# Gate and up of two SwiGLUs with tokens stationary, and six of their 32 weight sections in seven half-size products instead of eight

## The chip, the cores and the metric

One core of a Trainium2 chip runs the whole block as one launch. The metric is the device time of that core in microseconds, as the median of the runs.

## The reference

The block takes 256 tokens of width 1,024 in float32 and returns the same shape. It has three sub-layers, each with a norm before it and a norm of its output, which is then added to x:

```python
x = x + 0.5 * rmsnorm(swiglu(rmsnorm(x, ffn1_pre_g), w_gate, w_up, w_down), ffn1_post_g)
h = rmsnorm(x, mix_pre_g)
z = h @ w_in                       # q, k, v, f | u, v_s | gates a, b
o_a = forgetting_attention(q, k, v, f, b_forget)
o_b = spatial_gating(gelu(u), gelu(v_s), ...)
x = x + rmsnorm((sigmoid(ga) * o_a + sigmoid(gb) * o_b) @ w_out, mix_post_g)
x = x + 0.5 * rmsnorm(swiglu(rmsnorm(x, ffn2_pre_g), ...), ffn2_post_g)
```

`swiglu(h, w_gate, w_up, w_down)` is `(silu(h @ w_gate) * (h @ w_up)) @ w_down` with 4,096 columns in gate and in up. These two, the first and the second SwiGLU, are what the change is about.

## The kernel before, in words

**Products.** Every large product is made of three float32r products. `split` (L77) makes the two parts of an operand: ScalarE casts it to `hi` (L78), VectorE subtracts that from the source and writes `lo` (L79). TensorE then adds hi·hi, hi·lo and lo·hi in one PSUM bank.

**Weights.** `load` (L90) brings 1 MiB, 128 partitions by 2,048 columns, into one of three buffers of the pool `raws`; SP's queue issues it. `piece` (L97) splits 1,024 of these columns into a pair of the pool `wts` (11 pairs), and `unit` (L106) is a load with its two pieces.

**Tokens.** The 256 tokens are two token tiles of 128. `xT` (L64) holds the normed x, turned and split: [partition, K tile of 8, token tile, hi | lo, 128]. `to_xT` (L154) fills half the columns of one token tile, with four transposes on TensorE and a split of their PSUM bank.

**SwiGLU** (`ffn`, L220). The 4,096 columns are 32 F tiles of 128. For each, `gate_up` (L232) holds the weights stationary (`wide`, L189): per K tile one product of 512 columns (both token tiles, hi and lo) and one of 256. Gate and up come out with F on the partitions, so `swiglu` (L212) needs no transpose: it adds the two halves (`wide_sum`), applies silu, multiplies and splits the result into `hT`, four F tiles in a buffer of the pool `big`. `down` (L265) is the product with the down weights, 6 products of 512 columns for an F tile and token tile, added up over all 32 F tiles in four PSUM banks `y`. It comes one F tile later in TensorE's queue; for the last ten F tiles (`DEFER`) token tile 1 waits until token tile 0 is done, so that tile 0's norm runs beside tile 1's products, and of these two (`KEEP`) come after tile 0 is turned into `xT`.

In the second SwiGLU the first four F tiles (`LEAD`) are done by token tile (`gate_up_of`, L240) with tokens stationary and turned by two transposes each. The transposes that put token tile 1 into `xT` stand after 72 of tile 0's 96 products of 256 columns.

**Mixer.** `proj` (L316) holds tokens stationary and moves 512 columns of weights. `section` (L327) does 1,024 columns for both token tiles at a time, `section_by_tile` (L341) first for one tile and then for the other. `section_by_tile` is used for v, gb and wo, next to the places where a token tile's norm is still under way.

**Norms.** `post_norm` (L179) and `pre_norm` (L167) follow each other for a token tile: ScalarE squares the halves of y (L139), VectorE multiplies y by the gain (`yg`, L182), GpSimd adds the two sums (L144) and takes the power -1/2 (L146) for `r`, VectorE updates x (L186); then squares of x, `r` again, and `hn` (L164), which is turned into `xT`.

**Order.** Each engine runs its queue in order. The program is written as one sequence, with `later(n, fn)` and `tick()` (L118, L121) putting a step off by n chunks of other work, and the framework sets each engine's queue from it.

Of the kernel before, what the change touches and what calls it, by code (L numbers as in the profile page):

```python
# [22 lines left out]
P = 128  # L23
# [6 lines left out]
H = 8  # L30
# [4 lines left out]
DEFER = 10          # last F tiles whose down product waits for token tile 1 until token tile 0 is done  # L35
KEEP = 2            # of these, the ones that come after token tile 0 is put into xT
LEAD = 4            # F tiles of the second SwiGLU that are done by token tile
WARM = 14           # idle products before the first data are there
FORGET, SCORES, TURN = 5, 3, 3  # chunks of other work before these steps (see later)
# [3 lines left out]
def block(ctx: ExitStack, tc: tile.TileContext, a: dict, out: bass.AP):  # L43
    nc = tc.nc
    const = ctx.enter_context(tc.tile_pool(name="const", bufs=1))
    raws = ctx.enter_context(tc.tile_pool(name="raws", bufs=3))
    wts = ctx.enter_context(tc.tile_pool(name="wts", bufs=11))
    gains = ctx.enter_context(tc.tile_pool(name="gains", bufs=2))
    mid = ctx.enter_context(tc.tile_pool(name="mid", bufs=12))
    big = ctx.enter_context(tc.tile_pool(name="big", bufs=3))  # L50
    small = ctx.enter_context(tc.tile_pool(name="small", bufs=4))
# [29 lines left out]
    def in_order(instructions):  # L81
        """Each engine takes its instructions of the list in the list's order."""
# [14 lines left out]
    def piece(raw, j, name, trace=None):  # L97
        r = raw[:, j * 1024:(j + 1) * 1024]
        hi = wts.tile([P, 1024], F32R, tag="hi", name=f"hi_{name}_{j}")
        lo = wts.tile([P, 1024], F32R, tag="lo", name=f"lo_{name}_{j}")  # L100
        done = split(hi, lo, r)
        if trace is not None:
            trace.extend(done)
        return hi, lo

    def unit(src, name):  # L106
        """1 MiB of weights, split into two pieces of 1024 columns."""
        raw = load(src, name)
        return [piece(raw, j, name) for j in range(2)]

    def view(piece, **kw):
        (k, n), = kw.items()
        return [w.rearrange("p (k n) -> p k n", k=n) for w in piece]

# [39 lines left out]
    def to_xT(t, c, src, name):  # L154
        """Half of the columns of a token tile into xT."""
# [33 lines left out]
    def wide(ps, lhs):  # L189
        """lhs(k): (hi, lo) [128, 128]."""  # L190
# [19 lines left out]
    marks = {}  # L210

    def swiglu(gate, up, hT, name):  # L212
        g = wide_sum(gate, f"g{name}")
        sg = mid_tile([P, NT, P], f"sg{name}")
# [472 lines left out]
```

## Time and profile before

| | |
|---|---|
| median of three runs | 766.69 us (766.54 to 766.77) |
| profiled execution, span | 766.7 us |
| TensorE busy | 755.1 us (98%), 3,974 products |
| VectorE busy | 486.4 us (63%) |
| ScalarE busy | 413.2 us (54%) |
| GpSimd busy | 17.4 us (2%) |
| read from HBM | 140.02 MB, 184 GB/s over the span |

The page gives no time of its own for the profiled execution beside its span, so the span is set against the runs. A product of TensorE is shown from its start to its modelled end, and neighbours overlap, so the length of one product is not the pace. The pace is read from the chain of waits in order of time, where a run of products stands with the time that the run took.

### The profile page before, as it was taken

To read this page: it belongs to the slowest core of one execution; us is meant where nothing else is said; L and a number is where in the kernel's file an instruction comes from. 1 tells how busy PE (TensorE), PEld (TensorE's weight loads), DVE (VectorE), ACT (ScalarE), POOL (GpSimd) and SP (SyncE) were. 2 spreads that over 40 slices of the span, in tenths; PEclk is the share of its full clock that TensorE was granted. 3 is DMA by queue.
4 is the path that set the end of the run, shared out by engine and by line. 5 is a ranking of instruction groups with operands and counts; after the bars stand their busy time and mean duration, and the time that the engine had idled before them with its cause. 6 is when DMAs were issued, how large, how long until landed. Compare 5 with 4: busy or idle time off the path is not lost.

```text
span 766.7 us, 10137 instructions
## 1 busy us (share of the span) xinstructions
PE 755.1 (98%) x3974; PEld 641.4 (84%) x3974; DVE 486.4 (63%) x731; ACT 413.2 (54%) x655; POOL 17.4 (2%) x32
## 2 busy tenths in 40 slices
PE   7999999999999999999999999999999999999996
PEld 4888888888888878888888888898888888888885
DVE  5885665666566586755486646875666566565652
ACT  4865555554545585754544434754555555554441
POOL 1000000000000020000010000200000000000000
PEclk8999999999999999999999999999999999999999
DMA  7885455555444366633346725555455545544401
GB/s 287 309 316 222 169 215 180 205 171 215 165 165 143 136 219 221 236 136 140 115 160 196 273 84 216 196 219 217 165 194 193 205 177 194 191 167 163 165 1 55
DMA packets 21983, 141.72 MB, mean 185 GB/s; under 512 B 3184, under 2 KB 3440, under 8 KB 5680
## 3 DMA queue, kind: packets, MB, share of 16 engines
q1 hardware_dynamic: 21936, 141.08, 51.0%
q8 instruction: 31, 0.51, 0.3%
q14 instruction: 16, 0.13, 0.1%
HBM read 140.02 MB, written 1.05 MB: 184 GB/s over the span
## 4 chain that ended last, share of the span: by engine, by line
PE 97%; DMA 1%; ACT 0%; DVE 0%; POOL 0%; issue 0%; SPq 0%; DVEq 0%; POOLq 0%; ACTq 0%
PE y L274 22%; PE g L194 15%; PE u L194 14%; PE u L195 8%; PE g L195 7%; PE qk L194 4%; PE gu L250 3%; PE v L321 3%; PE ga L321 3%; PE sv L321 3%; PE wo L321 3%; PE gb L321 3%; PE u L321 3%; PE qk L195 2%; DMA g_ffn_pre_g<-in_ffn_pre_g 1%; PE tp_f L158 1%
## 5 line engine op out<-in xcount | busy, mean ns | idle before, releaser
L79 DVE TENSOR_TENSOR lo_g<-raw_g,hi_g 128x1024 fp32r<-128x1024 f32 x128 | 155.9, 1224 | 88.0 <-ACT hi_g L78 87.8
L78 ACT CAST hi_g<-raw_g 128x1024 fp32r<-128x1024 f32 x128 | 133.3, 1049 | 73.8 <-PE y L274 60.0
L194 PE MATMUL u<-xT,hi_g 128*128 128x512 f32 x480 | 171.4, 394 | 0.0
L194 PE MATMUL g<-xT,hi_g 128*128 128x512 f32 x480 | 171.2, 395 | 0.0
L274 PE MATMUL y<-hi_d,hT 128*128 128x512 f32 x512 | 148.7, 392 | 0.0
L195 PE MATMUL u<-xT,lo_g 128*128 128x256 f32 x480 | 135.9, 283 | 0.0
L195 PE MATMUL g<-xT,lo_g 128*128 128x256 f32 x480 | 135.0, 281 | 0.0
L79 DVE TENSOR_TENSOR lo_d<-raw_d,hi_d 128x1024 fp32r<-128x1024 f32 x64 | 78.1, 1225 | 48.7 <-ACT hi_d L78 48.7
L274 PEld LDWEIGHTS y<-hi_d,hT 128*128 128x128 f32 x512 | 92.1, 188 | 19.1
L194 PEld LDWEIGHTS g<-xT,hi_g 128*128 128x128 f32 x480 | 90.5, 188 | 20.7 <-ACT hi_g L78 0.3
L194 PEld LDWEIGHTS u<-xT,hi_g 128*128 128x128 f32 x480 | 90.3, 188 | 20.6
L195 PEld LDWEIGHTS g<-xT,lo_g 128*128 128x128 f32 x480 | 90.4, 188 | 3.1 <-DVE lo_g L79 0.8
L195 PEld LDWEIGHTS u<-xT,lo_g 128*128 128x128 f32 x480 | 90.2, 188 | 0.1
L274 PE MATMUL y<-lo_d,hT 128*128 128x512 f32 x256 | 80.0, 391 | 0.0
L78 ACT CAST hi_d<-raw_d 128x1024 fp32r<-128x1024 f32 x64 | 66.7, 1049 | 16.8 <-PE u L194 9.7
L201 ACT ACTIVATE low_g<-g 128x256 f32<-128x256 f32 x60 | 23.0, 383 | 72.5 <-PE g L195 72.4
L274 PEld LDWEIGHTS y<-lo_d,hT 128*128 128x128 f32 x256 | 48.1, 188 | 10.6
L204 DVE TENSOR_TENSOR s_g<-g,low_g 128x256 f32<-128x256 f32 x60 | 25.4, 424 | 33.3 <-ACT low_g L201 33.3
L78 ACT CAST hT<-s_u 128x256 fp32r<-128x256 f32 x60 | 24.1, 402 | 30.9 <-DVE s_u L217 30.8
L215 ACT ACTIVATE sg<-s_g 128x256 f32<-128x256 f32 x60 | 25.0, 417 | 27.2 <-DVE s_g L204 27.2
L79 DVE TENSOR_TENSOR hT<-s_u,hT 128x256 fp32r<-128x256 f32 x60 | 25.2, 420 | 8.4 <-ACT hT L78 8.2
L217 DVE TENSOR_TENSOR s_u<-sg,s_u 128x256 f32<-128x256 f32 x60 | 25.5, 425 | 1.9
(324 smaller groups left out, 985.7 us busy)
## 6 DMA issues: line engine op xcount, KB each, us to landing
raw_g<-in_gu SPq DMA_DIRECT2D x63, 1024.0 KB, 4.8
raw_d<-in_dn SPq DMA_DIRECT2D x32, 1024.0 KB, 4.8
x<-in_x SPq DMA_DIRECT2D x2, 512.0 KB, 3.8
raw_g<-in_gu SPq DMA_DIRECT2D x2, 512.0 KB, 8.6
g_ffn_post_g<-in_ffn_post_g SPq DMA_DIRECT2D x2, 512.0 KB, 8.8
raw_v0a<-in_w_v SPq DMA_DIRECT2D x1, 1024.0 KB, 4.7
raw_v0b<-in_w_v SPq DMA_DIRECT2D x1, 1024.0 KB, 4.8
raw_v1a<-in_w_v SPq DMA_DIRECT2D x1, 1024.0 KB, 4.8
```

What stands on the lines that cost most here:

```text
L78: return [nc.scalar.copy(out=hi, in_=src), nc.vector.tensor_tensor(out=lo, in0=src, in1=hi.bitcast(F32), op=ALU.subtract)]
L79: nc.vector.tensor_tensor(out=lo, in0=src, in1=hi.bitcast(F32), op=ALU.subtract)]
L158: nc.tensor.transpose(out=ps[:, i * P:(i + 1) * P], in_=src[:, i * P:(i + 1) * P], identity=ident)
L194: nc.tensor.matmul(ps, lhsT=hi, rhs=xT[:, k], start=k == 0, stop=False, skip_group_check=True)
L195: nc.tensor.matmul(top, lhsT=lo, rhs=xT[:, k, :, 0, :], start=False, stop=k == KT - 1, skip_group_check=True)
L201: nc.scalar.activation(out=low, in_=pv[:, :, 1, :], func=AF.Copy, scale=scale)
L204: nc.vector.tensor_tensor(out=s, in0=pv[:, :, 0, :], in1=low, op=ALU.add)
L215: nc.scalar.activation(out=sg, in_=g, func=AF.Silu)
L217: nc.vector.tensor_tensor(out=u, in0=sg, in1=u, op=ALU.mult)
L250: nc.tensor.matmul(ps[:, i * 256:(i + 1) * 256], lhsT=xT[:, k, t, xs, :], rhs=w, start=k == 0 and q == 0, stop=k == KT - 1 and q == 2, ski ...
L274: nc.tensor.matmul(ys[t][c], lhsT=hT[:, t, xs, :], rhs=w[:, c * 512:(c + 1) * 512], start=f == 0 and q == 0, stop=f == NF - 1 and q == 2)
L321: nc.tensor.matmul(ps, lhsT=xT[:, k, t, xs, :], rhs=w, start=k == 0 and q == 0, stop=k == KT - 1 and q == 2)
```

## The change

**Weights.** Gate and up come as blocks of 1,024 columns, four blocks (`NB`) of each, cut like the mixer's sections into quarters of 512 columns by half of K: `src[c, kh]`, 1 MiB each. `quarter` loads one and splits it in one step of 2,048 columns (`parts_of`), where `piece` took 1,024. The pool `raws` has five buffers in place of three, `wts` four pairs of 2,048 columns in place of 11 of 1,024.

**Products.** All of gate and up now hold tokens stationary, 512 columns to a product. For each block, gate is done first and then up. Gate of block 0 is done by token tile; the other sections are `section` or, for up of blocks 1 to 3 of both SwiGLUs (`FAST1`, `FAST2`), `fast`. `fast` takes the section as a 2 by 2 product: token tiles by column halves, with K in two halves. Where `section` makes eight products of one token tile, one quarter and half of K (12 matmuls each), `fast` makes seven, out of sums of quarters (`add`, in place in the raw buffers) and sums of parts of xT (`sums`, once for each SwiGLU), and puts the four results together with `mixed`. Both kinds of sums are on VectorE. The parts of xT's sums are split like any operand.

**Transposes.** h is now [tokens, columns]. For each block, token tile and column half, `turn` transposes it in four steps on TensorE and splits the result into `hT`.

**Order.** The down products of block b - 1 are spread over the steps of block b. The transposes of token tile 1 into `xT` in the second SwiGLU (`before`) come after two steps of block 0's gate, that is 24 products. In the first SwiGLU the last eight F tiles less two (`HOLD`) are done for tile 0 first and then for tile 1. At the start all four parts of xT are made before the first gate section, and its first quarter is split in two halves.

```diff
-    raws = ctx.enter_context(tc.tile_pool(name="raws", bufs=3))
-    wts = ctx.enter_context(tc.tile_pool(name="wts", bufs=11))
+    raws = ctx.enter_context(tc.tile_pool(name="raws", bufs=5))
+    wts = ctx.enter_context(tc.tile_pool(name="wts", bufs=4))
...
+    def sums(name):
+        kept = big.tile([P, NT, 2, 512], F32, tag="b", name=f"kept_{name}")
+        for t in range(NT):
+            for c in range(2):
+                hi, lo = [xT[:, c * 4:c * 4 + 4, t, i, :].bitcast(F32) for i in range(2)]
+                nc.vector.tensor_tensor(out=kept[:, t, c].rearrange("p (k c) -> p k c", c=P), in0=hi, in1=lo, op=ALU.add)
...
+    def fast(src, name, parts, done):
...
+        b11 = get(0, 0)
+        a = bank(f"{name}A")
+        product(a, lhs_x(0, 0), b11, "p1", True)
+        p1 = mid_tile([P, 512], f"{name}p1")
+        nc.scalar.copy(out=p1, in_=a)
+        yield
+        b12 = get(1, 0)
+        add(b11, b11, b12)
+        c = bank(f"{name}C")
+        product(c, lhs_s(0), b11, "p5", True)
+        yield
+        b22 = get(1, 1)
+        add(b11, b11, b22)
+        b = bank(f"{name}B")
+        product(b, lhs_s(1), b11, "p6", True)
+        u2 = mixed("u2", b, p1, ALU.add)
+        w = mixed("w", c, u2, ALU.subtract)
+        yield
+        add(b12, b12, b22)
+        b21 = get(0, 1)
+        product(a, lhs_x(1, 0), b21, "p2", False)
+        done(0, 0, a)
+        yield
+        d = bank(f"{name}D")
+        product(d, lhs_s(2), b12, "p7", True)
+        done(1, 1, mixed("y11", w, d, ALU.subtract))
+        yield
+        product(c, lhs_s(3), b22, "p3", False)
+        done(0, 1, mixed("y01", c, u2, ALU.subtract))
+        yield
+        add(b11, b11, b21)
+        product(d, lhs_x(1, 1), b11, "p4", False)
+        done(1, 0, mixed("y10", d, u2, ALU.add))
+        yield
...
+            for gen, _ in steps:
+                for _ in gen:
+                    at += 1
+                    if b == 0 and at == 2 and before:
+                        before()
+                    if b == 0 and at == 9 and quick:
+                        parts.append(sums(f"f{n}"))
+                    tick()
+                    while had > 0 and gone < had * at // total:
+                        f = side.pop(0)
+                        down(f, 0)
+                        down(f, 1)
+                        gone += 1
...
-    ffn(2, LEAD, done2, lambda t: turn[t]())
+    ffn(2, FAST2, done2, before=lambda: turn[1]())
```

The next three pieces are of the engines' queues, each row an instruction with its line, what it writes and reads, and the shape.

VectorE's queue in the middle of the first SwiGLU, before: F tiles 18 and 19, with gate and up weights `g1_22`, `g1_23` and down weights `d1_20` split beside them.

```order
L204 TENSOR_TENSOR s_g1_18_1535<-g1_18_1499,low_g1_18_1533 128x256
L79 TENSOR_TENSOR lo_d1_20_0_1767<-raw_d1_20_1764,hi_d1_20_0_1766 128x1024
L79 TENSOR_TENSOR lo_d1_20_1_1771<-raw_d1_20_1764,hi_d1_20_1_1770 128x1024
L204 TENSOR_TENSOR s_u1_18_1541<-u1_18_1500,low_u1_18_1539 128x256
L217 TENSOR_TENSOR s_u1_18_1541<-sg1_18_1537,s_u1_18_1541 128x256
L79 TENSOR_TENSOR lo_g1_22_0_1789<-raw_g1_22_1786,hi_g1_22_0_1788 128x1024
L79 TENSOR_TENSOR hT1_16_1384<-s_u1_18_1541,hT1_16_1384 128x2x128
L204 TENSOR_TENSOR s_g1_19_1604<-g1_19_1568,low_g1_19_1602 128x256
L79 TENSOR_TENSOR lo_g1_22_1_1793<-raw_g1_22_1786,hi_g1_22_1_1792 128x1024
L79 TENSOR_TENSOR lo_g1_23_0_1858<-raw_g1_23_1855,hi_g1_23_0_1857 128x1024
L204 TENSOR_TENSOR s_u1_19_1610<-u1_19_1569,low_u1_19_1608 128x256
L217 TENSOR_TENSOR s_u1_19_1610<-sg1_19_1606,s_u1_19_1610 128x256
```

The change puts in that engine's queue the beginning of up of block 2 (`lo_u1_2p1` to `u1_2w`):

```order
L84 TENSOR_TENSOR lo_u1_2p1_1106<-raw_u1_200_1102,hi_u1_2p1_1105 128x2048
L289 TENSOR_TENSOR raw_u1_200_1102<-raw_u1_200_1102,raw_u1_210_1123 128x2048
L289 TENSOR_TENSOR raw_u1_210_1123<-raw_u1_210_1123,raw_u1_211_1161 128x2048
L84 TENSOR_TENSOR lo_u1_2p5_1128<-raw_u1_200_1102,hi_u1_2p5_1127 128x2048
L289 TENSOR_TENSOR raw_u1_200_1102<-raw_u1_200_1102,raw_u1_211_1161 128x2048
L84 TENSOR_TENSOR lo_d1_12_1146<-raw_d1_12_1143,hi_d1_12_1145 128x2048
L84 TENSOR_TENSOR lo_u1_2p6_1166<-raw_u1_200_1102,hi_u1_2p6_1165 128x2048
L289 TENSOR_TENSOR raw_u1_200_1102<-raw_u1_200_1102,raw_u1_201_1186 128x2048
L84 TENSOR_TENSOR lo_u1_2p2_1189<-raw_u1_201_1186,hi_u1_2p2_1188 128x2048
L84 TENSOR_TENSOR lo_u1_2p7_1219<-raw_u1_210_1123,hi_u1_2p7_1218 128x2048
L293 TENSOR_TENSOR u1_2u2_1181<-u1_2B_1164,u1_2p1_1121 128x512
L293 TENSOR_TENSOR u1_2w_1183<-u1_2C_1126,u1_2u2_1181 128x512
```

Where subtractions of 1,024 columns stood between short steps of 256, there are now passes over 2,048 columns, seven subtractions and four sums to a section (the first four and three of them here), and the first two combinations `u2` and `w` stand behind five subtractions of the section and one of down weights.

VectorE's queue before, from the last subtractions of `g2_3` to token tile 1's `hn_f21` at the entry into the second SwiGLU (`xT` rows are tile 0's):

```order
L79 TENSOR_TENSOR lo_g2_3_0_4504<-raw_g2_3_4501,hi_g2_3_0_4503 128x1024
L79 TENSOR_TENSOR xT_82<-tp_f200_4365,xT_82 128x4x128
L79 TENSOR_TENSOR xT_82<-tp_f201_4372,xT_82 128x4x128
L79 TENSOR_TENSOR lo_g2_3_1_4508<-raw_g2_3_4501,hi_g2_3_1_4507 128x1024
L79 TENSOR_TENSOR lo_g2_4_0_4700<-raw_g2_4_4697,hi_g2_4_0_4699 128x1024
L182 SCALAR_TENSOR_TENSOR yg_pm11_4398<-wo11_4352,g_mix_post_g_4193 128x512
L186 SCALAR_TENSOR_TENSOR x_79<-yg_pm10_4396,r_pm1_4400,x_79 128x512
L186 SCALAR_TENSOR_TENSOR x_79<-yg_pm11_4398,r_pm1_4400,x_79 128x512
L79 TENSOR_TENSOR lo_g2_4_1_4704<-raw_g2_4_4697,hi_g2_4_1_4703 128x1024
L164 SCALAR_TENSOR_TENSOR hn_f210_4413<-x_79,r_f21_4410,g_ffn2_pre_g_4195 128x512
L164 SCALAR_TENSOR_TENSOR hn_f211_4415<-x_79,r_f21_4410,g_ffn2_pre_g_4195 128x512
```

And with the change, the same place:

```order
L184 SCALAR_TENSOR_TENSOR yg_pm10_3610<-wo10_3541,g_mix_post_g_3423 128x512
L84 TENSOR_TENSOR lo_g2_001_3642<-raw_g2_001_3639,hi_g2_001_3641 128x2048
L84 TENSOR_TENSOR xT_88<-tp_f200_3579,xT_88 128x4x128
L84 TENSOR_TENSOR xT_88<-tp_f201_3586,xT_88 128x4x128
L84 TENSOR_TENSOR lo_g2_010_3689<-raw_g2_010_3686,hi_g2_010_3688 128x2048
L184 SCALAR_TENSOR_TENSOR yg_pm11_3612<-wo11_3566,g_mix_post_g_3423 128x512
L188 SCALAR_TENSOR_TENSOR x_85<-yg_pm10_3610,r_pm1_3614,x_85 128x512
L188 SCALAR_TENSOR_TENSOR x_85<-yg_pm11_3612,r_pm1_3614,x_85 128x512
L84 TENSOR_TENSOR lo_g2_011_3695<-raw_g2_011_3692,hi_g2_011_3694 128x2048
L166 SCALAR_TENSOR_TENSOR hn_f210_3627<-x_85,r_f21_3624,g_ffn2_pre_g_3425 128x512
L166 SCALAR_TENSOR_TENSOR hn_f211_3629<-x_85,r_f21_3624,g_ffn2_pre_g_3425 128x512
```

A subtraction stands ahead of `yg_pm11` and another between the new x and `hn_f210` in both; with the change they are of 2,048 columns.

TensorE's queue before, around token tile 1's transposes `tp_f210` and `tp_f211` there:

```order
L250 MATMUL gu2_2_0_4511<-lo_g2_2_1_4498,xT_82 128x256
L250 MATMUL gu2_2_0_4511<-hi_g2_2_1_4497,xT_82 128x256
L158 MATMUL tp_f210_4536<-ident_83,hn_f210_4413 128x128 x4
L158 MATMUL tp_f211_4543<-ident_83,hn_f211_4415 128x128 x4
L250 MATMUL gu2_2_0_4511<-hi_g2_3_0_4503,xT_82 128x256
L250 MATMUL gu2_2_0_4511<-lo_g2_3_0_4504,xT_82 128x256
```

And with the change:

```order
L217 MATMUL g2_000_3645<-lo_g2_001_3642,xT_88 128x512
L217 MATMUL g2_000_3645<-hi_g2_001_3641,xT_88 128x512
L160 MATMUL tp_f210_3672<-ident_89,hn_f210_3627 128x128 x4
L160 MATMUL tp_f211_3679<-ident_89,hn_f211_3629 128x128 x4
L217 MATMUL g2_001_3698<-hi_g2_010_3688,xT_88 128x512
L217 MATMUL g2_001_3698<-lo_g2_010_3689,xT_88 128x512
```

The transposes keep their place behind token tile 0's products, but stand behind 24 of 512 columns in place of 72 of 256.

## Rows read from the trace of the kernel before

**Rows 1.** The page: busy time of each engine, and the chain by engine.
```profile
PE 755.1 (98%) x3974; PEld 641.4 (84%) x3974; DVE 486.4 (63%) x731; ACT 413.2 (54%) x655; POOL 17.4 (2%) x32
...
PE 97%; DMA 1%; ACT 0%; DVE 0%; POOL 0%; issue 0%; SPq 0%; DVEq 0%; POOLq 0%; ACTq 0%
```
**Rows 2.** Busy time by stretch: us, each engine (instructions), granted clock, DMA share, GB/s.
```profile
0.00:14.00 14.00, 9.35 (x31) 5.43 (x32) 6.31 (x14) 5.21 (x9) 1.92 (x8) 0.83 0.86 303
14.00:27.00 13.00, 12.96 (x67) 10.77 (x67) 10.44 (x14) 10.29 (x16) 0.00 (x0) 0.92 0.82 313
27.00:755.00 728.00, 727.27 (x3855) 620.98 (x3854) 466.86 (x701) 396.37 (x628) 14.62 (x22) 1.00 0.51 183
```
**Rows 3.** The chain in order of time: start us, us, engine, what, line, count.
```profile
26.50 2.75 PE y L274 x12
...
201.92 2.75 PE y L274 x12
...
271.50 0.24 ACT junk_p L139
...
443.84 16.73 PE gb L321 x72
...
487.40 0.87 PE tp_f L158 x8
...
491.06 8.65 PE gu L250 x72
...
500.59 2.85 PE gu L250 x24
...
503.66 5.70 PE gu L250 x48
```
**Rows 4.** Timeline, 10 to 15 us: start, us, engine, line, operation [idle before, releaser].
```profile
10.13 3.65 PE L158 MATMUL tp_f<-ident,hn_f 128*128 128x128 f32 x16 [3.44 <-DVE hn_f L164]
...
11.87 0.69 DVE L79 TENSOR_TENSOR xT<-tp_f,xT 128x512 fp32r<-128x512 f32 x1 [1.10 <-ACT xT L78]
...
13.69 0.79 PE L194 MATMUL g<-xT,hi_g 128*128 128x512 f32 x1
```
**Rows 5.** Groups by line and shape: busy us, mean ns of one, idle before.
```profile
L79 DVE TENSOR_TENSOR lo_g<-raw_g,hi_g 128x1024 fp32r<-128x1024 f32 x128 | 155.9, 1224 | 88.0 <-ACT hi_g L78 87.8
L78 ACT CAST hi_g<-raw_g 128x1024 fp32r<-128x1024 f32 x128 | 133.3, 1049 | 73.8 <-PE y L274 60.0 <-PE u L194 10.7 <-DMA raw_g<-in_gu 1.8
...
L79 DVE TENSOR_TENSOR xT<-tp_f,xT 128x512 fp32r<-128x512 f32 x8 | 5.2, 686 | 1.7 <-ACT xT L78 1.7
...
L78 ACT CAST xT<-tp_f 128x512 fp32r<-128x512 f32 x8 | 4.4, 590 | 7.7 <-PE tp_f L158 7.7
```
**Rows 6.** Timeline, GpSimd's step L144 and the VectorE subtractions beside it.
```profile
277.58 1.22 DVE L79 TENSOR_TENSOR lo_v1a<-raw_v1a,hi_v1a 128x1024 fp32r<-128x1024 f32 x1
277.79 1.19 POOL L144 TENSOR_SCALAR r_mx<-ms_mx 128x1 f32<-128x1 f32 x1 [3.84 <-ACT junk_mx L139]
...
289.53 0.30 POOL L144 TENSOR_SCALAR r_mx<-ms_mx 128x1 f32<-128x1 f32 x1 [2.46 <-ACT junk_mx L139]
...
490.93 2.35 DVE L79 TENSOR_TENSOR lo_g<-raw_g,hi_g 128x1024 fp32r<-128x1024 f32 x2
...
492.22 1.23 POOL L144 TENSOR_SCALAR r_pm<-ms_pm 128x1 f32<-128x1 f32 x1 [6.73 <-ACT junk_pm L139]
```
**Rows 7.** Timeline, VectorE and TensorE at the two entries.
```profile
279.65 1.42 DVE L164 SCALAR_TENSOR_TENSOR hn_mx<-x,r_mx,g_mix_pre_g 128x512 f32<-128x512 f32 x2 [0.84 <-POOL r_mx L146]
280.55 1.29 PE L158 MATMUL tp_mx<-ident,hn_mx 128*128 128x128 f32 x8 [0.70 <-DVE hn_mx L164]
...
485.53 1.42 DVE L164 SCALAR_TENSOR_TENSOR hn_f<-x,r_f,g_ffn_pre_g 128x512 f32<-128x512 f32 x2 [0.86 <-POOL r_f L146]
...
493.20 0.68 DVE L182 SCALAR_TENSOR_TENSOR yg_pm<-wo,g_mix_post_g 128x512 f32<-128x512 f32 x1
...
497.53 1.41 DVE L164 SCALAR_TENSOR_TENSOR hn_f<-x,r_f,g_ffn_pre_g 128x512 f32<-128x512 f32 x2 [0.85 <-POOL r_f L146]
```

More of the change, by code (lines that the diff above doesn't have):

```diff
@@ L95, in load, with parts_of, quarter @@
         return raw
[L97 to L103, printed above, removed]
-        return hi, lo
[L106 to L113, printed above, removed]
+    def parts_of(raw, name, parts=1, trace=None):
+        hi = wts.tile([P, 2048], F32R, tag="hi", name=f"hi_{name}")
+        lo = wts.tile([P, 2048], F32R, tag="lo", name=f"lo_{name}")
+        for c in range(0, 2048, 2048 // parts):
+            cs = slice(c, c + 2048 // parts)
+            done = split(hi[:, cs], lo[:, cs], raw[:, cs])
+            if trace is not None:
+                trace.append(done)
+        return hi, lo
+    def quarter(src, name):
+        return parts_of(load(src, name), name)
     pending = []
@@ new lines, in section_by_tile @@
+    def section_by_tile(src, name, done, first=None):
+        ws = {}
+        for t in range(NT):
+            for c in range(2):
+                for kh in range(2):
+                    if (c, kh) not in ws:
+                        ws[c, kh] = first if first and (c, kh) == (0, 0) else quarter(src[c, kh], f"{name}{c}{kh}")
+                ps = bank(f"{name}{t}{c}")
+                for kh in range(2):
+                    proj(ps, t, ws[c, kh], kh, 0, 1)
+                    if kh == 1:
+                        done(t, c, ps)
+                    yield
@@ L265, in down, with ffn @@
+    marks = {}
+    def ffn(n, quick, done, before=None, after=None, first=None):
+        gs, us, dn = a[f"g{n}"], a[f"u{n}"], a[f"dn{n}"]
+        hTs, ys, downs, sgs = {}, {}, {}, {}
         def down(f, t, cs=(0, 1)):
             if f not in downs:
-                downs[f], downs[f + 1] = unit(dn[f // 2], f"d{n}_{f}")
+                w = quarter(dn[f // 2], f"d{n}_{f}")
+                for i in range(2):
+                    downs[f + i] = [v[:, i * 1024:(i + 1) * 1024] for v in w]
             if t not in ys:
@@ L288, in ffn @@
-        late = []
-        nxt = 0
-        for f in range(lead, NF):
-            gate_up(f, first if (n, f) == (1, 0) else unit(gu[f], f"g{n}_{f}"))
-            if f == lead and lead:
-                turns[-1]()
-            while nxt < f:
-                down(nxt, 0)
-                if nxt < NF - DEFER:
-                    down(nxt, 1)
-                else:
-                    late.append(nxt)
-                nxt += 1
-        late.append(NF - 1)
-        down(late[0], 1)
-        down(late[1], 1)
@@ L305, in ffn @@
+        for f in side[:HOLD]:
+            down(f, 0)
+            down(f, 1)
+            tick()
+        late = side[HOLD:]
+        for f in late:
+            down(f, 0)
         done(0, ys[0])
-        for e in late[2:-KEEP]:
-            down(e, 1)
-        if n == 1:
-            turned(0)
+        for f in late[:-KEEP]:
+            down(f, 1)
+        if after:
+            after()
         for c in range(2):
-            for e in late[-KEEP:]:
-                down(e, 1, (c,))
+            for f in late[-KEEP:]:
+                down(f, 1, (c,))
@@ L476, in mixer, with columns @@
         kept = forget()
-        section_by_tile(a["w_v"], "v", v_done)
+        run(section_by_tile(a["w_v"], "v", v_done))
+        parts = sums("mx") if FASTM else None
+        def columns(src, name, done):
+            run(fast(src, name, parts, done) if name in FASTM else section(src, name, done))
         oA = attention(v, *kept)
-        ws = raws.tile([P, H, P], F32, tag="raw", name="ws")
+        ws = aux.tile([P, H, P], F32, tag="aux", name="ws")
         nc.vector.memset(ws[64:128, :, 0:64], 0.0)
@@ L526, in u_done @@
             later(2 + t, mix)
[L528 removed]
+        columns(a["w_u"], "u", u_done)
         def ga_done(t, c, ps):
@@ L577, in block @@
     nc.sync.dma_start(out=ident, in_=a["ident"])
-    trace, rs, first = [], [], []
+    trace, rs = [], []
     for t in range(NT):
```

235 lines of the change are left out of this document (119 added, 116 removed).

## The prediction

> **What bounds the kernel now.** First the page's busy shares and its chain of waits [rows 1]: TensorE is busy for 755.1 of 766.7 us and the chain lies on it for 97%, while VectorE is busy for 63% and ScalarE for 54%. Then the table by stretch [rows 2]: from 27 to 755 us TensorE is idle for 0.73 us in all, and its granted clock is 1.00, that is 2.4 GHz; in 0 to 14 and 14 to 27 it is lower. So a change counts by what it does to TensorE's queue, plus every wait that it opens there. Third, the chain in order of time [rows 3] gives the pace. From the y group of 12 at 26.50 to the one at 201.92 are 21 F tiles, 8.35 us each, 2.75 of which is the down product: gate and up of one F tile take 5.60 us. With tokens stationary, 72 products take 16.73 us, 232.4 ns each. The four F tiles done by token tile take 8.65 + 2.85 + 5.70 and once more 5.70, 22.9 us. Eight transposes take 0.87 us, 109 ns each.
>
> **TensorE, the matrix products.** Removed: 60 x 5.60 + 22.9 = 358.9 us. Added: ten sections of 96 products and six of 84, 1,464 products with tokens stationary, at 232.4 ns: 340.2 us. Sum: **-18.7**. The half-size products alone are six times 12 products, 16.7 us of it; the change of form is worth 2.0. Down products and the mixer's matrix products are the same in number.
>
> **TensorE, transposes.** h now comes out as [tokens, columns] and must be turned: 128 transposes in place of 8, so 120 x 109 ns = **+13.0**. They stand in TensorE's queue, which is full, so nothing hides them. Running sum: -5.7.
>
> **Start of the first SwiGLU.** Before, the first product starts at 13.69 [rows 4] and two F tiles are done at 26.50: 11.2 us of work, so the loss is 1.6 and the effective start 15.3. Now the first gate section runs token tile 0 over all four weight quarters, 12 products (2.8 us) each, and each quarter needs a 2,048-column split. VectorE's subtraction took 1.22 us for 1,024 columns and 0.69 for 512 [rows 5], 1.05 ns a column: 2.30 for 2,048. ScalarE's cast, 1.05 and 0.59: 1.95. On VectorE from 11.87 [rows 4], with the halves of the first quarter ready at about 14.1 and 16.0: two xT halves (17.2), one `kept` sum (17.9), a quarter (20.2), two sums (21.6), a quarter (23.9), a sum (24.6), the last quarter (26.9). After that 55 products are left, 12.8 us: the 96 products end at 39.7, less 22.3 of work is an effective start of 17.4, **+2.1**. Bounds: 0 if the sums yield, +4 if a load also comes late.
>
> **The two entries.** Here a token tile's norm stands between TensorE's last product and its next transposes, and VectorE's queue has a weight subtraction between x and hn in both kernels, twice as long now. It matters twice, because GpSimd's step waits too [rows 6]: r at L144 took 0.30 us alone, but 1.19 and 1.23 when a subtraction ran, ending 0.18 and 0.17 after that subtraction's own end (278.80 and 493.28).
> I take the hold to last to the subtraction's end, since both of these did; if it stayed at the 0.9 us that they cost, the entries below would be some 2 us cheaper in all.
> The Trainium skill (SBUF — State Buffer, section "Who interferes with whom") says that a VectorE instruction with two SBUF inputs and a GpSimd instruction that reads SBUF exclude each other for the whole instruction. The two rows agree with it; no run here shows a 2,048-column hold yet.
>
> Into the mixer: before, y's tile 0 ends at 271.50, hn starts at 279.65 and the transposes at 280.55 [rows 3, 7], with 36 y products (8.2 us) as cover and 0.70 us idle. Now the cast between the two squares is 0.9 longer, the subtraction then runs to about 280.2, r follows it, the transposes start near 281.8: **+1.3**.
>
> Into the second SwiGLU, tile 0: before, hn starts at 485.53 [rows 7] and the transposes are due at 487.40, so 1 us is to spare. Now the subtraction ends near 486.6, r at 487.4, hn at 488.15 and its second half at 488.85: +1.15.
> Tile 1: before, `wo` ends at 491.06, hn starts 6.5 us later, and 72 products of 8.65 us cover it [rows 3, 7]. Now `before()` is called after two steps, 24 products or 5.6 us. VectorE comes late to `yg_pm11` (it has hn, two quarters and two xT halves first, to 495.3, where before it was there at 493.20 [rows 7]); r is held until then, x is done at 497.4, the next subtraction at 499.65, r at 500.4, hn at 501.2. `wo` ends at 492.2 with the wait of tile 0, the 24 products at 497.8: idle 3.65. Together **+4.8**. Bounds: 2 (hold as in the rows, cast not in the way) to 7 (a 2.30 subtraction more).
>
> **The six seven-product sections.** VectorE has 11 passes over 2,048 columns (seven subtractions, four sums), 25.3 us, 13 passes over 512 columns (combinations, gate times up, hT) at 0.69, 9.0, and two down quarters, 4.6: 38.9 us. TensorE has 84 + 48 products and three groups of transposes there, 32.0. VectorE alone would be 6.9 us short in each. But it works ahead: by the order it runs five of the passes after the gate's last quarter and before the first weights that must wait for a buffer of this section, 11.5 us, and with four weight buffers and all four raw quarters loaded it can. So 27.4 remain against 32.0. The thin places are the transposes in and after the section, which wait for a combination that stands behind a subtraction: my walk leaves them 0.1 to 0.3 us. I take 0.4 a section, **+2.4**; the bounds are 0 and 6.9 a section, and the value lies near the low end because the cover is counted in the order.
>
> **Nothing:** ScalarE (seven casts of 1.95 and a copy in 32 us), the loads (same bytes; rows of the page show no product waiting for one after the start), the tail (same last products, same norm), and five buffers of raw weights for three. If VectorE is late, the first of these to bind is a load, since a raw quarter is freed by its last subtraction.
>
> **Sum:** -5.7 + 2.1 + 1.3 + 4.8 + 2.4 = +4.9. The profiled execution's span is 766.7, the runs' median 766.69, so the two need no correction: **771.6 us**, slower by 0.6%. About 0.2%, 1.5 us, is what a measurement of this kernel can tell from no change.
>
> **Rivals.**
> *Faster: the entries and sections wait for nothing more.* If the subtractions that stand before hn are done while VectorE would wait anyway, the terms 1.3, 4.8 and 2.4 go: 763.1. For it: ScalarE and VectorE have 46 and 37% idle, and the runs of before show no TensorE wait at the second entry. Against: the order puts the subtraction before hn. It decides where TensorE's idle time at the second entry is under 1 us.
> *VectorE is the bound in the seven-product sections.* If the lead is lost (a weight buffer or a raw quarter comes free late), up to 6.9 a section; with half of it, 6 x 3.5 = 21 more: 790. For it: 38.9 against 32.0. Against: the five passes ahead.
> *TensorE's clock falls in the new waits.* Rows: the clock is 0.83 in 0 to 14, where TensorE waits 3.44 us before its first transposes [rows 2, 4], 0.92 in 14 to 27 and then 1.00, also through the 0.70 us wait. At 0.92 over 13 us a wait costs 1.0 more; at the start and the second entry that is 2: 773.6, more if sections wait as well.
> The Trainium skill (TensorE: Matmul & The Clock Gate, section "HAM oscillation — how this bites in real kernels") states that idle gaps of TensorE bring its clock down and that each then starts cold; of the waits here, the trace shows it for the 3.44 us only, and for 0.70 us not.
> That the change doesn't do what it says is excluded: the order counts 504 products on the seven-product line.
>
> **How the numbers follow.** Forecast 0.56, of which the low ends (entries 3 to 4, sections 0 to 1, start 1: 765 to 767) leave 0.14 within 0.2%; faster rival 0.24; VectorE rival 0.13; clock 0.07. Faster 0.24, same 0.14, slower 0.62. The forecast's own range is 765 to 778; taking in most of the faster rival, down to a start that loses nothing more against 1 us left at the entries (762), and a small part of the VectorE rival (half a section in all, +3 on 778) gives 762 to 781.
>
> **What would show it.** Right: about 340 us of gate and up products at 232 ns, 128 transposes at 109 ns, TensorE idle some 3 to 4 us around the second entry with r at L146 as releaser one step back, and a few tenths per section before L371. Wrong: idle time of TensorE above 2 us in each seven-product section, waiting for VectorE's lo (the second rival); no idle at the entries (the first); a granted clock below 1.00 in the middle of the kernel (the third); or a pace of the 512-column products other than 232 ns, each nanosecond of which is 1.5 us.

## The result and the profile after

| | before | after |
|---|---|---|
| median | 766.73 us (766.54 to 766.98, 4 runs) | 771.93 us (769.38 to 773.91, 4 runs) |
| ratio | | 1.0061, 95% interval 1.0036 to 1.0085 |
| profiled execution | span 766.7 us | span 767.6 us, its time 769.38 us |

The change makes the kernel slower by 0.6%. The profiled execution is the fastest of the four. A run's time lies some 1.8 us above its span (769.38 and 767.6 here, 767.0 and 765.2 in a run of before beside the experiments), so the profiled execution of before, span 766.7, took about 768.5 us, 1.8 above the median of its runs. Two differences are therefore to be explained: 0.9 us between the two traces, and the rest between the trace of after and the median of its runs.

First the page of after, the busy time of each engine, against [rows 1]:

```profile
PE 746.9 (97%) x3446; PEld 608.1 (79%) x3446; DVE 539.0 (70%) x516; ACT 381.0 (50%) x376; POOL 21.5 (3%) x32
```

TensorE has 8.2 us less work than before and yet the span is longer: its idle time went from 11.6 to 20.7 us. Then the table by stretch, with the columns of [rows 2]:

```profile
0.00:14.00 14.00, 8.04 (x33) 4.06 (x34) 7.00 (x15) 6.22 (x11) 1.93 (x8) 1.00 0.88 305
14.00:27.00 13.00, 10.87 (x45) 7.93 (x44) 11.34 (x11) 8.14 (x7) 0.00 (x0) 1.00 1.01 424
27.00:755.00 728.00, 721.62 (x3344) 591.20 (x3343) 517.90 (x488) 365.26 (x356) 18.72 (x22) 1.00 0.49 180
```

Where before had 0.73 us idle between 27 and 755 us, after has 6.38. The timeline of TensorE names these waits, and ahead of them two waits for lo at the start: each row is the group that ended the wait, with the idle time and its releaser in brackets. The last four add up to 6.35 us.

```profile
13.45 0.50 PE L217 MATMUL g<-lo_g,xT 128*128 128x512 f32 x1 [0.77 <-DVE lo_g L84]
...
19.18 0.50 PE L217 MATMUL g<-lo_g,xT 128*128 128x512 f32 x1 [1.94 <-DVE lo_g L84]
...
279.84 0.63 PE L160 MATMUL tp_mx<-ident,hn_mx 128*128 128x128 f32 x4 [1.58 <-DVE hn_mx L166]
...
293.67 0.50 PE L217 MATMUL v<-lo_v,xT 128*128 128x512 f32 x1 [0.52 <-DVE lo_v L84]
...
488.21 1.23 PE L160 MATMUL tp_f<-ident,hn_f 128*128 128x128 f32 x8 [0.95 <-DVE hn_f L166]
...
501.14 1.29 PE L160 MATMUL tp_f<-ident,hn_f 128*128 128x128 f32 x8 [3.30 <-DVE hn_f L166]
```

Two of the rows are at the start, two at the entry into the mixer (token tile 0's transposes, then v's weights), two at the entry into the second SwiGLU (tile 0, tile 1). There is none in a seven-product section. The chain in order of time shows the pace there (start, us, what):

```profile
502.43 16.73 PE g L217 x72
...
576.48 2.80 PE u_1A L285 x12
...
590.27 2.75 PE y L350 x12
...
595.75 0.44 PE hp L371 x4
```

72 products in 16.73 us are 232 ns each, the pace of before [rows 3]; a half-size product of 12 takes 2.7 to 2.8 us, and four transposes of h 0.44, 109 ns each. All three are as forecast.

### The profile page after: what moved, and what is told of

It reads as the page before. It is cut to its first block, busy times and chain, and to the rows that moved or that the text cites. A ratio compares the mean times of both kernels' runs of the same rounds, so it can differ in the third digit from the quotient of the medians.

```text
span 767.6 us, 8470 instructions
## 1 busy us (share of the span) xinstructions
PE 746.9 (97%) x3446; PEld 608.1 (79%) x3446; DVE 539.0 (70%) x516; ACT 381.0 (50%) x376; POOL 21.5 (3%) x32
## 5 line engine op out<-in xcount | busy, mean ns | idle before, releaser
L217 PE MATMUL g<-hi_g,xT 128*128 128x512 f32 x512 | 166.7, 396 | 0.3 <-ACT hi_g L83 0.2
L217 PEld LDWEIGHTS g<-hi_g,xT 128*128 128x128 f32 x512 | 96.4, 188 | 23.1 <-ACT hi_g L83 1.0
L84 DVE TENSOR_TENSOR lo_g<-raw_g,hi_g 128x2048 fp32r<-128x2048 f32 (+1 forms) x33 | 73.4, 2225 | 44.9 <-ACT hi_g L83 44.9
L217 PE MATMUL g<-lo_g,xT 128*128 128x512 f32 x256 | 101.3, 396 | 2.8 <-DVE lo_g L84 2.7
L84 DVE TENSOR_TENSOR lo_d<-raw_d,hi_d 128x2048 fp32r<-128x2048 f32 x32 | 73.0, 2287 | 39.4 <-ACT hi_d L83 39.4
L83 ACT CAST hi_g<-raw_g 128x2048 fp32r<-128x2048 f32 (+1 forms) x33 | 61.2, 1856 | 34.7 <-PE u L217 10.5
L83 ACT CAST hi_d<-raw_d 128x2048 fp32r<-128x2048 f32 x32 | 60.8, 1915 | 26.9 <-PE g L217 8.8
L217 PE MATMUL u<-hi_u,xT 128*128 128x512 f32 x192 | 61.7, 396 | 0.0
L217 PEld LDWEIGHTS g<-lo_g,xT 128*128 128x128 f32 x256 | 48.3, 189 | 14.7 <-DVE lo_g L84 3.8
L289 DVE TENSOR_TENSOR raw_u<-raw_u,raw_u 128x2048 f32<-128x2048 f32 x24 | 55.0, 2292 | 0.8
L83 ACT CAST hi_u_3p<-raw_u 128x2048 fp32r<-128x2048 f32 x14 | 26.6, 1915 | 32.9 <-DVE raw_u L289 25.1
L84 DVE TENSOR_TENSOR lo_u<-raw_u,hi_u 128x2048 fp32r<-128x2048 f32 x12 | 27.4, 2289 | 16.6 <-ACT hi_u L83 16.5
```

Source lines behind the costliest of these rows:

```text
L83: return [nc.scalar.copy(out=hi, in_=src), nc.vector.tensor_tensor(out=lo, in0=src, in1=hi.bitcast(F32), op=ALU.subtract)]
L84: nc.vector.tensor_tensor(out=lo, in0=src, in1=hi.bitcast(F32), op=ALU.subtract)]
L217: nc.tensor.matmul(ps, lhsT=xT[:, kh * 4 + k, t, xs, :], rhs=v, start=kh == 0 and k == 0 and q == 0, stop=kh == 1 and k == 3 and q == 2)
L289: nc.vector.tensor_tensor(out=out, in0=p, in1=q, op=ALU.add)
```

## The experiments

Eleven runs follow, in groups of four, four and three. Each group had a chip of its own and the kernel before beside it, with medians of 768.36, 768.14 and 767.61 us, and each ratio is to the before of its group. Differences between edits are between medians; where the edits lie in different groups, before's own 0.2 to 0.8 us stands in them too. The first four runs are the changed kernel with no edit or one, the others stand on two of these edits.

**The change once more.** No edit.

> The changed kernel once more, nothing edited, to learn why its runs lie 4.5 us apart (769.4 to 773.9) where those of before lie within 0.5. Theory (the clock): the mean granted clock goes with the time (0.999 at 769.4, 0.989 at 773.9), so an execution with a longer time shows a stretch below 1.00 in its table by stretch, right after one of the new waits: after 19 us (wait of 1.94) or after 501 us (3.30); outside that stretch the idle times are those of the first trace within 0.2 us. Rival (other work varies): the clock rows stay at 1.00 and the idle time before some product is longer instead, by 1 to 4 us.

771.69 us (771.28 to 773.06, 5 runs), ratio 1.0050 (1.0033 to 1.0067): 3.3 us more than before, where the first measurement had 5.2. The span of its profiled execution is 769.9, 2.3 us more than in the first trace. The table by stretch around the wait of 3.33 us (it ends at 501.86):

```profile
502.00:504.00 2.00, 1.97 (x12) 1.52 (x12) 2.00 (x4) 1.17 (x2) 0.00 (x0) 0.84 0.89 291
504.00:506.00 2.00, 2.00 (x6) 1.59 (x5) 1.98 (x4) 0.00 (x0) 0.00 (x0) 0.50 0.47 197
506.00:508.00 2.00, 2.00 (x8) 1.60 (x7) 0.00 (x0) 0.00 (x0) 0.00 (x0) 0.80 0.00 0
```

and the same place in the first trace of after:

```profile
504.00:506.00 2.00, 2.00 (x11) 1.60 (x10) 1.26 (x3) 0.00 (x0) 0.00 (x0) 1.00 0.09 37
```

After the wait TensorE ran for some 3 us at clock 0.50, that is 1.2 GHz, in this execution, and at 2.4 GHz in the first. The price: from those transposes to the end are 767.6 - 501.14 = 266.5 us in the first trace and 769.9 - 501.86 = 268.0 here, 1.6 more. The other 0.7 us arose at the start: the first up section begins at 39.39 us in place of 38.66. There too the clock was low in this execution, 0.56 from 10 to 16 us, and 1.00 in the first. The same 16 transposes, here and in the first trace:

```profile
10.21 3.65 PE L160 MATMUL tp_f<-ident,hn_f 128*128 128x128 f32 x16 [3.94 <-DMA ident<-in_ident]
...
9.83 2.15 PE L160 MATMUL tp_f<-ident,hn_f 128*128 128x128 f32 x16 [3.78 <-DMA ident<-in_ident]
```

The waits themselves are the same within 0.3 us. So the clock theory holds, but in two places, and the one at the start, behind the wait before the first transposes, it had not named.

**Eight products everywhere.**

```diff
-FAST1 = {(b, "u") for b in range(1, NB)}
-FAST2 = {(b, "u") for b in range(1, NB)}
+FAST1 = set()
+FAST2 = set()
```

> The change of form alone: no seven-product section, all 32 sections in eight products. Theory: the six sections give back all that they save, 72 products of 232 ns, 16.7 us, since the trace shows TensorE with no idle time in them; the time rises by 16 to 17 us, to 786 in an execution at clock 1.00. Rival (VectorE holds the seven-product sections back): the saving is smaller than its products, the time rises by under 12.

788.29 us, ratio 1.0270 (1.0247 to 1.0293): 16.6 us above the change (16.3 between the spans of the two traces), and 72 products are 16.7. The six sections give all of it. It also sets apart what the other half of the change does: with the form alone, the kernel is 2.7% slower than before.

**Transposes one step later.**

```diff
-                    if b == 0 and at == 2 and before:
+                    if b == 0 and at == 3 and before:
```

> Only the transposes of token tile 1 at the entry into the second SwiGLU stand one step later, after 36 products in place of 24. Theory: 12 products are 2.8 us, so the wait of 3.30 us falls to 0.5 and the time by 2.8, to 766.6 in an execution at clock 1.00; the split of xT still has the 12 products of the fourth step as cover. If the low clock comes after this wait, the runs also draw together, within 1.5 us. Rival (the wait moves): xT's split is late for the first product of tile 1 and the wait comes back there, the time changes by less than 1.

767.88 us (766.33 to 768.62, 10 runs), ratio 0.9993 (0.9983 to 1.0002): 3.8 us less than the change, for one digit. TensorE's timeline, the row that had 3.30:

```profile
502.73 1.23 PE L160 MATMUL tp_f<-ident,hn_f 128*128 128x128 f32 x8 [0.54 <-DVE hn_f L166]
```

and the table by stretch behind it:

```profile
504.00:506.00 2.00, 2.00 (x10) 1.60 (x9) 2.00 (x4) 0.58 (x1) 0.00 (x0) 1.00 0.71 295
```

The wait gives 2.8 us, and the clock keeps 2.4 GHz behind the shorter one: from tile 0's transposes to the end this trace has 276.5 us and that of the change again 281.0, so 1.7 of the 4.5 are the clock's. Some 0.8 is lost again ahead of the mixer: at the start this execution was at 0.57 and 0.58 from 20 to 24 us, behind a wait of 2.21. The runs did not draw together as far as expected (2.3 us apart).

**Norm ahead of the splits.** `ahead` takes two entries for token tile 0: (last square, second half of hn), then the split of xT. The next two weight splits are queued behind them.

```diff
             done = split(hi[:, cs], lo[:, cs], raw[:, cs])
+            if ahead:
+                for late, early in zip(done, ahead.pop(0)):
+                    in_order([early, late])
```

> Queue order only, at both entries for token tile 0: the first weight split after a norm has its cast behind the norm's last square on ScalarE and its subtraction behind hn on VectorE, and the second split stands behind that of xT. Theory (the split ahead of hn makes the wait): r at L146 takes 0.3 us in place of 1.78, hn starts some 2.5 us earlier, the waits of 1.58 (mixer) and 0.95 us (second SwiGLU, tile 0) go; the one of tile 1 stays near 3.3: 2.5 us less, 767 in an execution at clock 1.00. Rival (the wait moves): the split that was put back is late for the first products that use it, and TensorE waits 1 to 2.5 us there for lo; the time stays within 1.

769.49 us, ratio 1.0021 (1.0010 to 1.0032): 2.2 less. The transposes of tile 0 wait at neither entry. What decides is seen in the timeline of the first trace of after, at the entry into the mixer: VectorE's subtraction, GpSimd's step L146, then hn.

```profile
275.80 2.29 DVE L84 TENSOR_TENSOR lo_v<-raw_v,hi_v 128x2048 fp32r<-128x2048 f32 x1 [1.99 <-ACT hi_v L83]
276.49 1.78 POOL L146 TENSOR_SCALAR r_mx<-ms_mx 128x1 f32<-128x1 f32 x1 [4.12 <-ACT junk_mx L141]
...
278.94 1.41 DVE L166 SCALAR_TENSOR_TENSOR hn_mx<-x,r_mx,g_mix_pre_g 128x512 f32<-128x512 f32 x2 [0.85 <-POOL r_mx L148]
```

The step runs until 278.27, the subtraction until 278.09. With the edit, the same step of GpSimd in its timeline:

```profile
275.78 0.30 POOL L151 TENSOR_SCALAR r_mx<-ms_mx 128x1 f32<-128x1 f32 x1 [2.46 <-ACT junk_mx L146]
```

The rival is true in part: behind this entry waits for v's lo (0.78 in place of 0.52) and for tile 1's transposes (0.63, new) take a piece back.

**Both edits.**

> Both edits of queue order together: token tile 1's transposes one step later at the second entry, and the first two splits behind tile 0's norm at both entries. Theory (the waits are of queue order alone, and add): of the 6.3 us of waits before transposes at the entries some 0.6 (tile 1 of the mixer) and 0.8 before v's lo are left, nothing at the second entry, and no stretch below clock 1.00 after 30 us; 771.7 less 3.8 less some 2 is 765.5 to 766.5, under the kernel before. Rival (the two edits are worth the same wait): no more than the better of them, 767.9.

766.69 us (765.51 to 767.73, 11 runs), ratio 0.9983 (0.9974 to 0.9992). 5.0 us less than the change (4.8 if each is set against the before of its group), where the parts add to 6.0. No stretch after 30 us is below clock 1.00, as expected, but the second entry has two waits that had not been foreseen, both for lo.

```profile
498.93 0.50 PE L227 MATMUL g<-lo_g,xT 128*128 128x512 f32 x1 [1.01 <-DVE lo_g L84]
503.39 0.50 PE L227 MATMUL g<-lo_g,xT 128*128 128x512 f32 x1 [0.54 <-DVE lo_g L84]
```

**Half steps at the start**, on top of both.

```diff
-        return parts_of(load(src, name), name)
+        return parts_of(load(src, name), name, 2 if name in ("g1_001", "g1_010", "g1_011") else 1)
```

> On top of both edits: the second to fourth weight quarters of the first gate section are split in two steps of 1,024 columns. Theory (the trace's reading of the start): the wait of 1.8 to 2.2 us before the second quarter's lo comes from a cast of 1.90 and a subtraction of 2.29 that stand one behind the other after the load, so half steps let TensorE start after 1.05 + 1.22; the wait falls by 1 to 1.5 us and the time with it, 0.8 to 1.5 less than with both edits. Rival (the prediction's reading): the sums kept ahead of the subtractions make the wait, they stay where they are, and the time changes by less than 0.5.

764.65 us, ratio 0.9958 (0.9942 to 0.9973), 2.0 less, somewhat more than expected. The wait in the first gate section fell from 2.29 to 0.67 us:

```profile
18.10 0.50 PE L227 MATMUL g<-lo_g,xT 128*128 128x512 f32 x1 [0.67 <-DVE lo_g L84]
```

The run changes more than it set out to: VectorE now took both half subtractions ahead of the first of xT's sums, where the trace of both edits has the sum first. VectorE with both edits, then with the half steps:

```profile
16.69 0.68 DVE L268 TENSOR_TENSOR kept_f<-xT 128x512 f32<-128x512 f32 x1
17.29 2.29 DVE L84 TENSOR_TENSOR lo_g<-raw_g,hi_g 128x2048 fp32r<-128x2048 f32 x1
...
16.83 2.35 DVE L84 TENSOR_TENSOR lo_g<-raw_g,hi_g 128x1024 fp32r<-128x1024 f32 x2
19.10 0.68 DVE L268 TENSOR_TENSOR kept_f<-xT 128x512 f32<-128x512 f32 x1
```

With both edits the cast was done at 16.80, so the sum held the subtraction back by 0.5 us (in the two traces of the change by 0.15 and 0.5). The other 1.1 of the 1.6 us is the length of a cast and a subtraction over 2,048 columns in a row. The two spans, 765.7 and 762.8, differ by more than the wait, and that fits the clock: with the wait of 2.29 the trace shows 0.50 from 20 to 22 us, with 0.67 it stays at 1.00.

**Up of block 0 in seven products too**, on top of both: `FAST1` and `FAST2` over `range(NB)`, with the sums one step earlier.

> On top of both edits: up of block 0 in both SwiGLUs in seven products as well, eight sections in place of six. Theory (what six sections gave, two more give: no down weights are split in block 0, so VectorE has 25 us of passes and 9 of short ones there, and the sums of xT's parts, against 42 of TensorE for gate and up): 24 products, 5.6 us less than with both edits, 760. Rival (VectorE or the loads are the bound at the start of a SwiGLU): TensorE waits in the section for lo, for parts of xT or for a load, and the time falls by less than 3.

791.80 us, ratio 1.0306 (1.0292 to 1.0320): 25.1 us *more* than both edits, not 5.6 less. In TensorE's timeline the new section waits six times in each SwiGLU, 9.6 us in the first; the longest:

```profile
51.27 0.80 PE L295 MATMUL u_0B<-hi_u_0p,parts_f 128*128 128x512 f32 x1 [5.24 <-ACT hi_u_0p L83]
```

and in the table by stretch VectorE is busy for 9.23 of 10 us, then the clock is down:

```profile
40.00:50.00 10.00, 5.54 (x22) 3.67 (x20) 9.23 (x11) 3.62 (x7) 0.00 (x0) 0.95 0.00 0
50.00:60.00 10.00, 7.72 (x18) 5.60 (x19) 8.00 (x5) 6.62 (x4) 0.00 (x0) 0.53 0.09 18
```

The expectation had set VectorE's passes against gate and up together. The section by itself has 34 us of VectorE, and the sums of xT's parts, against 84 products, 19.5 us, with no down products between them. VectorE did not work ahead: it stood idle for 8.54 us until 33.06, since the section's first cast came only when products of the gate section by token tile were done, which by the code keeps all four weight buffers. And the wait of 5.24 us is one of queue order: from 39.93 to 46.95 VectorE was mostly at xT's sums and their split, which this edit puts into the section, and the weight sum that the cast needed came behind them. No run takes one of the three (no down products, no work ahead, xT's sums) away by itself. The six waits of each SwiGLU, 19.1 us in all, less the 5.6 of products saved are 13.5; the low clock is some 9 of the other 11.6, an estimate from the granted clock of the stretches below 1.00.

**The mixer's sv, u and ga in seven products**, on top of both: `FASTM = {"sv", "u", "ga"}`.

> On top of both edits: the mixer's sections sv, u and ga in seven products, with sums of xT's parts for the mixer. Theory (VectorE's capacity sets where it pays): VectorE is busy for 15 of 20 us in sv and u and 10 in ga already; four sums more and one subtraction less, combinations of 0.69 in place of nothing, are some 10 us more for each against 19.5 of TensorE: VectorE is short by 6 in sv and in u, TensorE waits for lo and for combinations, and the time is 0 to 9 us above that of both edits. Rival (VectorE's lead covers it, as in the six sections): 36 products less, 8.4 us below both edits.

796.99 us, ratio 1.0381 (1.0366 to 1.0395), 30.3 more than both. The direction is the theory's, the size is beyond its range. TensorE waits 14 times from sv to gb, 25.6 us in all, mostly for hi and lo of a sum; the longest wait and the table by stretch:

```profile
407.70 0.79 PE L295 MATMUL uC<-hi_up,parts_mx 128*128 128x512 f32 x1 [8.39 <-ACT hi_up L83]
```

```profile
400.00:420.00 20.00, 7.34 (x17) 4.73 (x18) 18.20 (x33) 8.12 (x6) 2.08 (x2) 0.62 0.15 53
```

25.6 less the 8.4 of products saved are 17.2; the clock, 0.62 here and 0.83 from 440 to 460 us, had been left out of the expectation too. Whether it is the whole of the other 13 us isn't shown.

**Sums behind the first gate section**, on top of both and the half steps.

```diff
-                        parts.append(sums(f"f{n}"))
+                        with tc.issue_after(last[-1][1].ins):
+                            parts.append(sums(f"f{n}"))
```

> On top of both edits and the half steps: the sums of xT's parts are queued on VectorE behind the last subtraction of the first gate section, in both SwiGLUs. Theory: two of them (1.28 us) stand ahead of the second quarter's subtraction at the second entry, where TensorE waits 1.01 and 0.54 us for lo; behind it they hold nothing, since the first seven-product section comes 55 us later; 1 to 1.5 us less than with the half steps, 763.2 to 763.7, and 0.3 of it at the start at most. Rival (lo is late for the cast, not for the sums): the waits stay, 764.6.

763.67 us (762.59 to 764.64, 6 runs), ratio 0.9950 (0.9937 to 0.9962). It is the fastest kernel here, 0.5% under before, some 7 to 8 us under the change. The gain over the half steps, 1.0 us (0.5 if each is set against the before of its group), is within what their intervals leave open; the waits for lo at the start and at the second entry are gone from the trace, and TensorE's timeline has three waits after the start:

```profile
289.62 0.50 PE L229 MATMUL v<-lo_v,xT 128*128 128x512 f32 x1 [0.78 <-DVE lo_v L84]
291.22 0.66 PE L167 MATMUL tp_mx<-ident,hn_mx 128*128 128x128 f32 x4 [0.64 <-DVE hn_mx L173]
...
499.02 0.63 PE L167 MATMUL tp_f<-ident,hn_f 128*128 128x128 f32 x4 [0.73 <-DVE hn_f L173]
```

**Three and seven more passes.** On top of both and the half steps, to measure the room that VectorE has in a seven-product section: some subtractions are done twice.

```diff
             w = parts_of(raw, f"{name}{nm}")
+            if nm in ("p2", "p7", "p3",):
+                nc.vector.tensor_tensor(out=w[1], in0=raw, in1=w[0].bitcast(F32), op=ALU.subtract)
```

> On top of both edits and the half steps: three of the seven subtractions of each seven-product section (p2, p7, p3) are done twice on VectorE, which changes no value and adds 3 x 2.29 = 6.9 us to VectorE in each of six sections. Theory (VectorE's room is that of the block of 67 us, in which it is busy for some 51): nothing, within 1 us. Rival (the prediction's count, 27.4 of 32.0 us in the section): the section has room for 4.6 and is short by 2.3, 6 x 2.3 = 14 more.

> The same with all seven subtractions of each section done twice, 16.0 us more of VectorE in each. Theory (room of the block): 51 + 16 = 67 of 67, just full; short by what the order wastes, 0 to 4 us a section, 0 to 24 more. Rival (room of the section): 27.4 + 16.0 - 32.0 = 11.4 a section, 68 more.

786.05 us, ratio 1.0239 (1.0222 to 1.0257), and 844.74 us, 1.1004 (1.0985 to 1.1024): 21.4 and 80.1 more than with the half steps alone, 3.6 and 13.3 for each section on the average, out of 6.9 and 16.0 us that were added. The theory (room of the block) falls; the prediction's count (14 and 68 more) has the direction and comes out too low.

The average hides that the three sections of a SwiGLU differ. In the first SwiGLU, from the first product of a block's up to that of the next, and from block 3's to the mixer's first transposes, the half steps alone have 65.4, 62.7 and 54.0 us, three passes 67.4, 64.5 and 62.0, seven passes 76.8, 74.9 and 71.8. So of the 6.9 us added, blocks 1 and 2 pay 2.0 and 1.8, which leaves some 5 us of room, near the prediction's 4.6, and of the 16.0 they pay 11.4 and 12.2. Block 3 pays 8.0 and 17.8, all that was added and more: it had next to no room. In the trace of the half steps VectorE goes on behind block 3's section with the subtractions of five down quarters, from 250.28 to 263 us; that this is the reason was not tested.

Where the three passes are felt, in TensorE's timeline of the first SwiGLU's blocks 2 and 3:

```profile
184.09 0.50 PE L297 MATMUL u_2C<-lo_u_2p,parts_f 128*128 128x512 f32 x1 [1.16 <-DVE lo_u_2p L293]
...
240.38 0.50 PE L297 MATMUL u_3A<-lo_u_3p,xT 128*128 128x512 f32 x1 [1.71 <-DVE lo_u_3p L293]
...
256.78 0.63 PE L383 MATMUL hp<-ident,sg 128*128 128x128 f32 x4 [1.60 <-DVE sg L375]
258.97 1.55 PE L362 MATMUL y<-hi_d,hT 128*128 128x512 f32 x3 [1.30 <-ACT hi_d L83]
```

and, for the unchanged sections, the table by stretch of the first trace of after, block 2's gate and then its up:

```profile
132.00:165.00 33.00, 33.00 (x145) 26.85 (x144) 20.34 (x11) 14.21 (x12) 0.00 (x0) 1.00 0.33 110
165.00:198.00 33.00, 33.00 (x154) 27.03 (x153) 31.26 (x24) 19.27 (x14) 0.00 (x0) 1.00 0.74 277
```

VectorE is busy for 31.26 of 33 us in the up half without TensorE losing anything, and for 20.34 in the gate half. The room of the gate half was not there for the passes that were added to the up half; that the buffers set how far VectorE can work ahead is argued from the code. The 21.4 us is more than the waits of that trace (16.3 us over both SwiGLUs). The clock falls here too, to 0.50 from 260 to 262 us, behind the two waits in the last rows, and at the same place of the second SwiGLU; that is some 3 us of it, an estimate from the granted clock, and the rest isn't accounted for.

## Why the prediction was right, and where it was not

The forecast was 771.6 us, slower by 0.6%, and the median is 771.93. The sign and the mechanism hold: what the products save is spent on transposes and on waits of queue order at the start and the entries. But that the two numbers meet to 0.3 us is luck: errors of both signs cancel in the sum, and beside the before of its own group the change cost 3.3 us, where the forecast had 4.9 and the first measurement 5.2. By its steps:

- **Products -18.7, transposes +13.0.** Held. The half-size products are worth their 16.7 us (16.6 with eight everywhere); 109 ns a transpose and 232 ns a product are in the chain. The change of form, 2.0 of the 18.7, was not measured by itself.
- **Start +2.1.** The first up section starts at 38.66 us in the first trace and at 39.39 in the second; less the 22.3 us of 96 products, the effective starts are 16.4 and 17.1, against 15.3: +1.1 and +1.8. The size nearly held. The reason given for it, the `kept` sums ahead of the splits, did not: behind the first quarter each trace has one wait, for the second quarter's lo, and none for the last quarter, where the sum put it; the sums held that lo back by 0.15 and 0.5 us of the 1.94 and 2.19, and the rest is a cast and a subtraction of 2,048 columns one behind the other, which half steps shortened.
- **Mixer +1.3.** Measured 1.58 - 0.70 = +0.9 before the transposes, and 0.52 before v's lo, which no step of the prediction had. The size is met by two waits where one was named.
- **Second entry +4.8.** Measured 0.95 + 3.30 = 4.25, by the mechanism that was named, to 0.4 us in each tile. GpSimd's step was held to the end of the subtraction, as [rows 6] had it for half that length: here and at the mixer it ended 0.16 to 0.18 us behind it, and for tile 0 it took 1.78 us, not the 1.2 of the shorter subtraction. The Trainium skill (SBUF — State Buffer, section "Who interferes with whom") says that a VectorE instruction with two SBUF inputs contends with a GpSimd instruction that reads SBUF. This trace agrees with it, by these 1.78 us.
- **Sections +2.4.** This step failed: no wait in any of the six. The count behind it, 27.4 of 32.0 with 4.6 us of room, is near the truth for blocks 1 and 2, where some 5 were measured, and not for block 3, which had next to none; the 0.4 a section put on top of it, for transposes that come late, was not there.
- **The clock.** It was a rival with a chance of 0.07, and it came on top of the forecast: 1.6 us behind the 3.3 us wait in the second trace. How often it came is an estimate from the mean granted clocks. By the table by stretch of the second trace, whose mean is 0.991, the stretch at the start takes 0.0044 off the mean and the one behind the wait 0.0022; the first trace, with neither, has 0.999. So a mean of 0.994 (two of the nine runs) is what the start alone leaves, and the 0.989 to 0.991 of six runs need the wait's stretch as well; only two of the nine have a trace. The step that failed is that the sum took the clock as 1.00 through the waits, from a wait of 0.70 us.
- **"The two need no correction."** This failed too. Time is span + 1.8, so the profiled execution of before lay 1.8 us above the median. (Its clock at the start is in the last section. Among the executions of before beside the experiments, the five with a mean clock of 0.998 have spans of 764.0 to 765.2, the thirteen at 0.993 have 765.9 to 767.1. That fits, but that the clock makes the whole 1.8 is not shown.)

Against the trace of before the sum of the measured terms is -5.7 + 1.1 + 0.9 + 0.5 + 4.25 = +1.0, and the spans differ by 0.9. With the start of the second trace, +1.8, and the clock, +1.6, it is +3.3, and the spans differ by 3.2; and from the first median of before, 1.8 under its trace, that is 5.1 of the 5.2 measured. On the chip of the second trace before's median, 768.36, stands for a span of 766.6, about that of the trace of before, and there 3.3 us are what was measured. The rival of VectorE as the bound was wrong for the six sections. In block 0 and in the mixer, one section further, TensorE did wait for VectorE's queue.

## What to carry to other kernels

Seven products for eight pay where VectorE's passes fit beside TensorE's products: here each of six sections with down products in it saved its 2.8 us, with some 5 us of VectorE's room in two blocks and next to none in the third, and sections without them cost 10 to 13 us instead. Those sections also had other passes of VectorE in them (in block 0 xT's sums, and no work ahead), so how much is due to the missing down products alone is not shown. Count the room for each section alone, not for a longer stretch and not as an average. When an operation on a shared queue becomes longer, look at every place where a norm or another short chain passes through the same queue: one digit in the place of eight transposes was worth 3.8 us of the 7 to 9 that the new waits and their clock cost.

## What was not expected of the hardware

- Behind a wait of 2.9 to 3.3 us TensorE ran at half clock for some 3 us in three of four traces (the change again, eight products, norm first), and in the fourth, the first trace of after, it did not; behind single waits of up to 1.58 us at the entries it never did. At the start, behind waits of 1.6 to 2.3 us, it did so in three traces (one step later, both edits, block 0) and not in five. Behind two waits of 1.60 and 1.30 us, which ended 2.2 us apart, it ran at half clock as well (three more passes).
- Such a stretch at the start comes in some executions and not in others: the profiled execution of before was at 0.50 from 10 to 16 us, the change again at 0.56, and the first trace of after, which did the same transposes, at 1.00.
